# Which two loads have plain rows: the first batch's or the last batch's

## The chip, the cores and the metric

One core of a Trainium2 chip runs the kernel. The metric is device time in microseconds, lower is better.

## The reference

```python
def setup_inputs():
    batch, m, k, n = 16, 512, 768, 1024
    return {"x": np.random.randn(batch, k, m).astype(np.float32),
            "y": np.random.randn(batch, k, n).astype(np.float32)}

def reference(x, y):
    return np.einsum('bkm,bkn->bmn', x, y).astype(np.float32)
```

Sixteen matrix products in float32; the kernel reads 75.50 MB and writes 33.55 MB.

## The kernel before

SyncE issues every transfer, on one queue: 16 loads of x (1.5 MB each), 16 of y (3 MB) and 16 stores (2 MB). VectorE casts what has landed to bf16, TensorE multiplies, ScalarE copies from PSUM to the output buffers. Loads have two buffers each, so the load of batch b waits for the cast of batch b - 2.

The part that the change touches is the form of a load. Rows of x are 12 KB per partition in HBM and lie one behind the other, so four partitions' rows make one run of 48 KB; for y, two rows of 24 KB do. A **plain** load names 128 rows on both sides; a **wide** one names 32 or 64 source runs of 48 KB and still 128 destination rows. The ordinary call makes a plain load; the wide ones are built by hand from it:

```python
    made = {}
    def wide_dma(key, dst, src, dram_rows, load):
        if key not in made:                       # batch 0: plain rows
            made[key] = nc.sync.dma_start(dst, src)
            return made[key]
        pat = mybir.BassSymbolicTensorAccessPattern
        widen = lambda a: a.rearrange("(q r) k m -> q (r k m)", r=dram_rows)
        plain = lambda a: a.rearrange("p k m -> p (k m)")
        s, d = (widen(src), plain(dst)) if load else (plain(src), widen(dst))
        return nc.sync.add_instruction(_copy.replace(
            made[key].ins, name=nc.get_next_instruction_name(),
            ins=(...), outs=(...), sync_info=None, ant_dge_precooked=False))
    ...
    def load(b):
        i = b % 2
        if b >= 2:
            nc.sync.wait_ge(cast, nx[b - 2])
        wide_dma("x", xs[i][:], x_v[b], 4, True).then_inc(sx[i], 16)
        if b >= 2:
            nc.sync.wait_ge(cast, nx[b - 2] + parts(b - 2))
        wide_dma("y", ys[i][:], y_v[b], 2, True).then_inc(sy[i], 16)
    ...                                           # cut
```

## Time and profile before

| what | before | from |
|---|---|---|
| time, median of the runs beside the changed kernel | 260.73 us (260.63 to 260.77) | runs |
| span in the profile | 259.0 us | page |
| share of the 16 DMA engines, main queue | 98.5% | page, part 3 |
| busiest compute engine: PE | 69% | page, part 1 |
| first issue: start, duration | 0.95, 0.39 us | timeline |
| first packet of any engine starts | 1.97 us | packet records |
| x, then y of batch 0 done on the middle engine | 6.54, 13.87 us | packet records |
| last data packet ends | 257.72 us | packet records |
| x of batch 0, y of batch 0, last store complete, mean of the 16 engines | 6.49, 13.85, 256.44 us | packet records |

How to read it: "page" is the printed summary of a profile; its lines and the timeline are shown and read in the prediction. The last rows place the streams of packets in time, one stream on each of the 16 DMA engines; the middle engine is the one in the middle of the 16 by time. The packet records list each DMA packet's start, size and duration; no view prints them, so they stand here as numbers. Each engine closes each transfer with a completion packet of 4 bytes, and the times of completion are those of these packets.

### The profile page before, as it was taken

The page shows a single profiled execution, that of the slowest core. Times are in us where ns is not written, and L with a number is a line of the kernel's source. Part 1 is how long each engine was busy: PE and PEld are TensorE (multiplying, and loading weights), DVE is VectorE, ACT ScalarE, POOL GpSimd, SP SyncE. Part 2 cuts the span into 40 slices and gives each one's busy share as a digit, 9 for nine tenths or more (in the row PEclk, how much of TensorE's full clock was granted, in tenths as well). Part 3 has the DMA queues.
Part 4 walks back from the last instruction along what each step waited for, and adds up shares of the span by engine and source line. Part 5 has one row for each costly group of instructions (what it writes and reads, how often), then busy time and mean ns, then how long its engine had stood idle before and what let it go on. Part 6 is the DMA issues. An engine that isn't in the chain of part 4 may idle for free. (4 is left out here: it accounts for less than half of the span.)

```text
span 259.0 us, 2506 instructions
## 1 busy us (share of the span) xinstructions
PE 179.0 (69%) x768; PEld 88.9 (34%) x768; DVE 82.0 (32%) x33; ACT 60.9 (24%) x33; POOL 0.2 (0%) x4
## 2 busy tenths in 40 slices
PE   0009999999999006999069999595008999969500
PEld 0004555554545002454025555252003555534200
DVE  0261645527164350002245263300242536410000
ACT  1000342244220005222202241433000234052300
POOL 0000000000000000000000000000000000000000
PEclk9999999999999855899759999999555999988965
DMA  7999989899999999999999998999999999999995
GB/s 270 428 490 395 471 380 478 380 471 395 456 402 448 387 428 425 433 463 456 410 440 410 440 448 377 435 423 463 471 387 471 395 456 410 395 428 438 423 435 240
DMA packets 4514, 109.07 MB, mean 421 GB/s; under 512 B 768, under 2 KB 768, under 8 KB 768
## 3 DMA queue, kind: packets, MB, share of 16 engines
q1 hardware_dynamic: 4512, 109.05, 98.5%
q14 instruction: 2, 0.02, 0.0%
HBM read 75.50 MB, written 33.55 MB: 421 GB/s over the span
## 5 line engine op out<-in xcount | busy, mean ns | idle before, releaser
L154 PE MATMUL ps<-yb,xb 128*128 x768 | 179.0, 397 | 64.3 <-PEq L149 64.3
L154 PEld LDWEIGHTS ps<-yb,xb 128*128 x768 | 88.9, 116 | 154.0 <-issue 82.6
L170 ACT COPY ob<-ps 128x2048 f32<-128x2048 f32 x32 | 59.6, 1872 | 179.0 <-PE ps L154 139.9
L132 DVE CAST yb<-ys 128x6144 bf16<-128x6144 f32 (+1 forms) x17 | 53.8, 3171 | 77.2 <-DMA ys<-in_y_dram 77.2
L128 DVE CAST xb<-xs 128x3072 bf16<-128x3072 f32 x16 | 28.2, 1760 | 68.3 <-DMA xs<-in_x_dram 53.7
L170 ACT ACT_TABLE_LOAD x1 | 1.3, 1283 | 5.3 <-issue 5.3
L200 POOL MEMSET const-bfloat16-1.0<- 128x1 bf16 x1 | 0.1, 103 | 0.0
L200 POOL MEMSET const-uint8-127<- 128x1 uint8 x1 | 0.1, 103 | 0.0
L200 POOL MEMSET const-float32-0.0<- 128x1 f32 x1 | 0.1, 99 | 0.2 <-issue 0.2
L200 POOL MEMSET const-float32-1.0<- 128x1 f32 x1 | 0.1, 99 | 0.0
## 6 DMA issues: line engine op xcount, KB each, us to landing
ys<-in_y_dram SPq DMA_DIRECT2D x16, 3072.0 KB, 18.6
out_dram<-ob SPq DMA_DIRECT2D x16, 2048.0 KB, 26.3
xs<-in_x_dram SPq DMA_DIRECT2D x16, 1536.0 KB, 20.1
```

Source lines behind the costliest of these rows:

```text
L128: nc.vector.tensor_copy(xb[:, i], xs[i][:]).then_inc(cast, 1)
L132: nc.vector.tensor_copy(yb[:, i, ks], ys[i][:, ks]).then_inc(cast, 1)
L154: mm = nc.tensor.matmul(ps[g][:, m, nt], x_w[:, bass.ds(s, 1), kt, mo], yb[:, bass.ds(s, 1), kt, nt * NF:(nt + 1) * NF], start=(kt == 0), ...
L170: cp = nc.scalar.copy(ob[b % NO][:, g * HB:(g + 1) * HB].rearrange("p m (t f) -> p m t f", f=NF), ps[g][:])
L200: nc = _bacc.Bacc("TRN2", target_bir_lowering=False, num_devices=1)
```

## The change

Its intent is to let the very first loads have 48 KB runs too. Two plain loads must remain, and they become those of the last batch.

```diff
-    made = {}
-    def wide_dma(key, dst, src, dram_rows, load):
-        if key not in made:
-            made[key] = nc.sync.dma_start(dst, src)
-            return made[key]
+    def load_dma(b, dst, src, rows):
+        if b == B - 1:
+            return nc.sync.dma_start(dst, src)
+        s = src.rearrange("(q r) k m -> q (r k m)", r=rows)
+        d = dst.rearrange("p k m -> p (k m)")
         pat = mybir.BassSymbolicTensorAccessPattern
...                                               # cut
+        return nc.sync.add_instruction(mybir.InstDMACopy(
+            mode="Copy", name=nc.get_next_instruction_name(),
+            engine=nc.sync.engine, queue="qSPDynamicHW",
             ins=(...), outs=(...)))
...                                               # cut
-        wide_dma("x", xs[i][:], x_v[b], 4, True).then_inc(sx[i], 16)
+        load_dma(b, xs[i][:], x_v[b], 4).then_inc(sx[i], 16)
```

More of the change, by code (lines that the diff above doesn't have):

```diff
@@ L3 @@
 _os.environ.setdefault("NEURON_RT_ULTRASERVER_MODE", "4")
-import copy as _copy
 from contextlib import ExitStack
@@ L65 @@
     outs = ec(nc.semaphore("outs"))
-    made = {}
-    def wide_dma(key, dst, src, dram_rows, load):
-        if key not in made:
-            made[key] = nc.sync.dma_start(dst, src)
-            return made[key]
-        pat = mybir.BassSymbolicTensorAccessPattern
-        widen = lambda a: a.rearrange("(q r) k m -> q (r k m)", r=dram_rows)
-        plain = lambda a: a.rearrange("p k m -> p (k m)")
-        s, d = (widen(src), plain(dst)) if load else (plain(src), widen(dst))
-        return nc.sync.add_instruction(_copy.replace(
-            made[key].ins, name=nc.get_next_instruction_name(),
+    def load_dma(b, dst, src, rows):
[3 more added lines that the diff above has]
+        d = dst.rearrange("p k m -> p (k m)")
+        pat = mybir.BassSymbolicTensorAccessPattern
+        return nc.sync.add_instruction(mybir.InstDMACopy(
+            mode="Copy", name=nc.get_next_instruction_name(),
+            engine=nc.sync.engine, queue="qSPDynamicHW",
             ins=(pat(ap=s.ap, dtype=s.dtype, bass_ap=s, is_dma=False),),
-            outs=(pat(ap=d.ap, dtype=d.dtype, bass_ap=d, is_dma=False),),
-            sync_info=None, ant_dge_precooked=False))
+            outs=(pat(ap=d.ap, dtype=d.dtype, bass_ap=d, is_dma=False),)))
     def parts(b):
@@ L106, in load @@
             nc.sync.wait_ge(cast, nx[b - 2])
-        wide_dma("x", xs[i][:], x_v[b], 4, True).then_inc(sx[i], 16)
+        load_dma(b, xs[i][:], x_v[b], 4).then_inc(sx[i], 16)
         if b >= 2:
             nc.sync.wait_ge(cast, nx[b - 2] + parts(b - 2))
-        wide_dma("y", ys[i][:], y_v[b], 2, True).then_inc(sy[i], 16)
+        load_dma(b, ys[i][:], y_v[b], 2).then_inc(sy[i], 16)
     loads, stores = iter(range(B)), iter(range(B - 1))
```

## The prediction

> **What bounds the kernel now.** I read the page first, for who is busy. Its first, second and third parts answer at once:
>
> ```profile
> PE 179.0 (69%) x768; PEld 88.9 (34%) x768; DVE 82.0 (32%) x33; ACT 60.9 (24%) x33; POOL 0.2 (0%) x4
> ...
> DMA  7999989899999999999999998999999999999995
> GB/s 270 428 490 395 471 380 478 380 471 395 456 402 448 387 428 425 433 463 456 410 440 410 440 448 377 435 423 463 471 387 471 395 456 410 395 428 438 423 435 240
> DMA packets 4514, 109.07 MB, mean 421 GB/s; under 512 B 768, under 2 KB 768, under 8 KB 768
> ...
> q1 hardware_dynamic: 4512, 109.05, 98.5%
> ```
>
> No compute engine is busy for more than 69% of the 259.0 us span, while the 16 DMA engines are busy for 98.5% of it; the only slices under 8 tenths are the first (7) and the last (5). The chain that ended last is of no use here: it covers 5% PE and 1% ACT, because it follows instructions and the end of this kernel is a transfer. The packet counts also tell how the transfers are cut. There are 48 transfers and 768 = 48 x 16 tiny packets, so each transfer runs on all 16 engines and ends with one completion write on each. The other 4512 - 768 = 3744 are data: 16 stores x 128 rows of 16 KB = 2048; batch 0, loaded with plain rows, 128 of 12 KB (x) and 128 of 24 KB (y) = 256; the 15 other batches, with 48 KB source runs, 32 (x) and 64 (y) each = 1440. The sum fits exactly.
>
> Next, the timeline of the first and the last microseconds, for the transfer instructions (SPq). Columns: start, duration, what.
>
> ```profile
> 0.95 0.39 SPq L74 DMA_DIRECT2D xs<-in_x_dram  x1
> 1.39 0.42 SPq L74 DMA_DIRECT2D ys<-in_y_dram  x1
> 1.86 0.54 SPq L74 DMA_DIRECT2D xs<-in_x_dram  x1
> 2.44 0.65 SPq L74 DMA_DIRECT2D ys<-in_y_dram  x1
> ...
> 7.14 1.76 DVE L128 CAST xb<-xs 128x3072 bf16<-128x3072 f32 x1 [7.14 <-DMA xs<-in_x_dram]
> 8.93 0.47 SPq L74 DMA_DIRECT2D xs<-in_x_dram  x1
> 15.05 3.36 DVE L132 CAST yb<-ys 128x6144 bf16<-128x6144 f32 x1 [6.14 <-DMA ys<-in_y_dram]
> 18.43 0.47 SPq L74 DMA_DIRECT2D ys<-in_y_dram  x1
> ```
> ```profile
> 223.98 3.43 DVE L132 CAST yb<-ys 128x3072 bf16<-128x3072 f32 x2 [3.51 <-DMA ys<-in_y_dram]
> ...
> 243.33 1.87 ACT L170 COPY ob<-ps 128x2048 f32<-128x2048 f32 x1 [3.26 <-PE ps L154]
> 249.08 0.33 SPq L185 DMA_DIRECT2D out_dram<-ob  x1
> ```
>
> The reader should see four loads issued back to back, then one more each time a cast frees a buffer. Is the queue ever empty? The trace also lists each DMA packet with its start, size and duration; I strung them together into 16 serial streams, one an engine. On the middle engine every later transfer was issued 9 us or more before the engine reached it (the load of y for batch 2: issued by 18.90, reached at 28.43). Only the last store is closer: issued by 249.41, reached at 251.47. The streams have no hole but a few of 0.3 us beside instruction fetches. So **the end is the start of the first packet plus the length of one in-order stream per engine**, about 255 us. First packets start at 1.97 us (the last engine's at 2.80), last data packets end between 255.8 and 257.7 us.
>
> **What the Trainium skill says.** (1) "DMA: Bandwidth & Descriptors", section "Queues, rings and completion order": on each engine, descriptors are consumed in ring order. The trace agrees: the streams follow the order of issue. (2) Same page, "How many engines (k)", under the section on why a DMA adds 16 to its semaphore: the largest k up to 16 that divides the slowest dimension of both patterns. 32 and 64 source rows against 128 partitions still give 16, and the 768 completion writes agree, so the wide form loses no engine. (3) Same page, "Why small descriptors are slow": a fixed overhead of about 3 cycles per packet inside the DMA engine. The packet records show a fixed part: median 460 ns for 12,288 B and 912 ns for 24,576 B, a straight line with 452 ns per 12,288 B and 8 ns fixed. It predicts 8 + 4 x 452 = 1816 ns for 49,152 B; the undisturbed ones take 1815. At these sizes 8 ns is 2% at most. (4) Same page, "Specifications": about 0.6 us to the first byte for a transfer issued from SP. Here the first issue ends at 0.95 + 0.39 = 1.34 and the first packet starts at 1.97: 0.63 us.
>
> **The change part by part.** The order of instructions stays: 48 transfers on one queue with the same waits. Nothing else moves on any engine. What differs is two plain loads, which go from the first two places to the last two load places, and two wide ones, which go the other way. The totals of packets of each size are the same.
>
> - Batch 0 becomes wide. Per engine, x goes from 8 x 460 = 3.68 us to 2 x 1.815 = 3.63 us; y from 8 x 912 = 7.30 to 4 x 1.815 = 7.26. Saved: 0.05 + 0.04 = **0.09 us**, at the head of every stream, so on the path.
> - Batch 15 becomes plain. The wide packets there have a median of 1829 ns, so 6 x 1.829 = 10.97 us now. Plain packets in the same mode: some of batch 0 that ran beside 1841 to 1848 ns wide ones took 465 and 920 ns, so 8 x 0.465 + 8 x 0.920 = 11.08. Added: **0.11 us**, ahead of the last six stores, so on the path too.
> - The first issue. Plain loads took 0.39 and 0.42 us to issue, unhurried wide ones 0.47. The first packet can only come after its issue: **+0.08 us**. For batch 15 issue time is hidden: the queue is over 9 us ahead.
> - The start. The 128 packets of 12 KB have a mean of 530 ns against a median of 460, all of it in the first two rounds (first packets 0.66 to 1.32 us). (530 - 460) x 128 / 16 = **0.56 us** per engine is start-up. If it is a latency, one per engine, the wide form pays the same once and the change is 0. If it is paid per packet, two wide packets pay about as much as the two first plain ones. I take 0, with 0.3 us either way.
>
> Sum: -0.09 + 0.11 + 0.08 + 0 = +0.10 us on 260.71: 260.8 us.
>
> What lies beside other work: x of batch 0 lands for the cast at 7.14 and would do so within 0.2 us; TensorE starts after y of batch 0 and its cast, at 18.99. Even half a microsecond there would be worth nothing, as no load waits that closely on the compute. At the end, the last ACT copy is done at 243.33 + 1.87 = 245.20, and the last store is issued at 249.08: 3.9 us of slack for a later landing of batch 15.
>
> **The rivals.**
> 1. *Wide runs start the kernel faster, and this shows.* For it: fewer, longer source reads in the phase in which all 16 engines start cold, and 0.56 us is lost there. Against: that is all there is to win. Halved: -0.3 us, so 260.4; none left: 260.2, a 0.2% gain.
> 2. *Wide runs start it slower.* A 48 KB packet can start only when the engine has its descriptors, and starts are staggered from 1.97 to 2.80 us already. If the stagger doubles, +0.8 us at most on the late engines, but those are not the ones that end last: +0.4, so 261.1.
> 3. *A wait at the end takes over.* Plain rows let the last y land differently, and the casts, matmuls and stores of batch 15 come later. The 3.9 us above speaks against it, as does that the store of batch 9 and not the load frees ACT at 228.87. It would take a landing 4 us late. Time: unchanged.
> 4. *Uneven engines.* One engine ends at 257.7 and the median at about 256.4; the slow one lost about 1 us in scattered hiccups beside instruction fetches and completions. Longer packets at the time of the early fetches could shift who is late: 0.5 us either way, and that is also the noise between executions of one kernel in one profile. The three timed runs spread over 0.14 us only.
>
> **Range and chances.** The sure terms are tenths of a microsecond and cancel; the unsure ones are the start (0.3) and the unevenness (0.4), together about 0.5. Range 260.3 to 261.3. 2% would be 5.2 us; nothing in the trace has that size except a queue that runs dry, and it is at least 9 us ahead. So within 2%: 0.98.
>
> **What would show it.** Right: the same 4514 packets with 98% or more DMA share; first packets at about 2.05 us; the first x cast at 7.0 to 7.3 and the first y cast at 14.8 to 15.3; issue of the first load 0.47 us; the last y cast within 0.3 us of 223.98; the last store issued within 0.5 us of 249.08. Wrong: first packets of 48 KB that take well over 1.8 + 0.6 us; a first cast that moves by over 0.5 us and an end that moves with it; plain packets at the end slower than 465 and 920 ns; or a hole in the streams.

## More of the kernel before

In the built program, what the ordinary call makes (plain loads and stores) carries a flag, `ant_dge_precooked`; what is built by hand does not. Below, a transfer with the flag is called *marked*.

## The result, and the profile after

The changed kernel takes **261.18 us** (261.15 to 261.30, four runs) against 260.73 us before: +0.45 us by the medians, a ratio of 1.0019 with an interval of 1.0001 to 1.0036. Ratios here are the mean time of one kernel's fast runs over that of the other's fast runs of the same rounds, so not quite the ratio of the medians. The result is in the predicted range of 260.3 to 261.3 and in the class "within 2%", and the loss is over four times the predicted 0.10 us.

The page of the changed kernel, busy times, packet counts and queue:

```profile
PE 178.6 (69%) x768; PEld 88.9 (34%) x768; DVE 82.0 (32%) x33; ACT 60.9 (23%) x33; POOL 0.2 (0%) x4
...
DMA packets 4515, 109.07 MB, mean 420 GB/s; under 512 B 769, under 2 KB 769, under 8 KB 769
...
q1 hardware_dynamic: 4512, 109.05, 98.4%
```

The main queue has the same 4512 packets and the same bytes (the one more packet is on the queue for instructions), and nearly the same share of a slightly longer span. So next to nothing was added to the streams; they lie later. The timeline of the changed kernel shows where, at the head (columns: start, duration, instruction):

```profile
0.95 0.55 SPq L75 DMA_DIRECT2D xs<-in_x_dram  x1
1.55 0.57 SPq L75 DMA_DIRECT2D ys<-in_y_dram  x1
2.17 0.60 SPq L75 DMA_DIRECT2D xs<-in_x_dram  x1
2.81 0.61 SPq L75 DMA_DIRECT2D ys<-in_y_dram  x1
...
7.77 1.76 DVE L123 CAST xb<-xs 128x3072 bf16<-128x3072 f32 x1 [7.77 <-DMA xs<-in_x_dram]
9.56 0.47 SPq L75 DMA_DIRECT2D xs<-in_x_dram  x1
15.44 3.36 DVE L127 CAST yb<-ys 128x6144 bf16<-128x6144 f32 x1 [5.90 <-DMA ys<-in_y_dram]
```

and at the tail:

```profile
196.72 0.35 SPq L71 DMA_DIRECT2D xs<-in_x_dram  x1
...
205.55 0.34 SPq L71 DMA_DIRECT2D ys<-in_y_dram  x1
...
224.15 3.43 DVE L127 CAST yb<-ys 128x3072 bf16<-128x3072 f32 x2 [4.85 <-DMA ys<-in_y_dram]
...
249.53 0.33 SPq L180 DMA_DIRECT2D out_dram<-ob  x1
```

The first issue starts at 0.95 as before and takes 0.55 us instead of 0.39. The first cast of y starts 0.39 us later (15.44 against 15.05), the last store is issued 0.45 us later (249.53 against 249.08), the span is 0.4 us longer. By the packet records, the first packet starts at 2.28 instead of 1.97 us. Averaged over the 16 engines, x of batch 0 is complete at 6.93 instead of 6.49 us, y of batch 0 at 14.29 instead of 13.85 and the last store at 256.86 instead of 256.44: 0.43 to 0.45 us later at each. A shift that is whole after the first transfer and no larger at the end was made at the head. (Single casts show it less well, as each waits for the slowest engine of its transfer: the last cast of y is only 0.17 us later, 224.15 against 223.98.)

### The profile page after: what moved, and what is told of

It is laid out like the page before. It is cut to its first block, busy times and chain, and to the rows that moved or that the text cites. A ratio compares the mean times of both kernels' runs of the same rounds, so it can differ in the third digit from the quotient of the medians.

```text
span 259.4 us, 2506 instructions
## 1 busy us (share of the span) xinstructions
PE 178.6 (69%) x768; PEld 88.9 (34%) x768; DVE 82.0 (32%) x33; ACT 60.9 (23%) x33; POOL 0.2 (0%) x4
## 3 DMA queue, kind: packets, MB, share of 16 engines
q1 hardware_dynamic: 4512, 109.05, 98.4%
```

## The experiments

My theory after this comparison, **H**: the time was lost ahead of the first packets and kept to the end, because no stream is ever empty. Its rivals: **T**, the plain rows of the last batch cost it; **C**, compute starts later and never catches up. H itself splits: **H1**, the form of the issue (marked or not) delays the start; **H2**, the 48 KB runs do. Ten kernels were run: nine ask a question, and the last is a version meant to be faster. All gave correct results, each was timed in five rounds beside the kernel before on the same chip. Kernels are compared only within the same rounds. The expectations name absolute times, so a few were missed by up to 0.11 us (experiments 1, 2, 4, 9 and 10); what counts is the difference from the kernel before.

### 1. Plain rows at both ends

```diff
# against the changed kernel
-        if b == B - 1:
+        if b in (0, B - 1):
```

> Batches 0 and 15 both plain, the rest wide. Theory H (the 0.45 us are lost at the head of the streams, before the first packets): 260.7 to 260.85, first packet at 1.97, middle engine done with x of batch 0 at about 6.5. Rival T (the plain rows of the last batch cost it): 261.1 to 261.2.

Measured: 260.65 us against 260.57, ratio 1.0002 (0.9989 to 1.0016); first packet at 1.97 us, x of batch 0 done at 6.58. The plain rows of the last batch alone cost nothing that can be seen. T falls.

### 2. The plain batch in the middle

A kernel without any plain load did not build: the compiler refused the hand-made load of y with "physical tensor cannot be Function argument and cannot be NEFF IO". I read this as each input needing one ordinary load somewhere, and that is why the change moves the plain rows and does not drop them. So they went to batch 7.

```diff
# against the changed kernel
-        if b == B - 1:
+        if b == 7:
```

> Batch 0 wide as in the changed kernel, last batch wide as in the kernel before, the one plain batch is number 7. Theory H: 261.1 to 261.25, first packet at 2.28. Rival T: 260.7 to 260.8.

Measured: 261.00 us against 260.57, ratio 1.0015 (1.0002 to 1.0029); first packet at 2.28 us. With the tail wide as it was before the change, the loss is still there. Together with the first experiment: the head makes it, the tail does not.

### 3. Plain rows at the head, without the mark

```diff
# against the kernel before
+    nc.dge_precook = False          # ordinary calls make unmarked transfers
     ...                             # cut
     for nl, ns in TURNS:
         for b in islice(loads, nl):
             load(b)
+            nc.dge_precook = True   # from the second batch on as before
```

> The kernel before, plain rows in batch 0, but the two first loads are issued without the mark that plain loads carry in the built program, as the wide ones are. Splits theory H. H1 (the form of the issue delays the start): issue about 0.55 us, first packet at about 2.25, time 261.05 to 261.2. H2 (the 48 KB runs delay it): issue 0.39 or a little more, first packet at 1.97 to 2.05, time 260.7 to 260.8.

Measured: 261.09 us against 260.57, ratio 1.0020 (1.0006 to 1.0034). Its timeline:

```profile
0.94 0.54 SPq L74 DMA_DIRECT2D xs<-in_x_dram  x1
1.54 0.58 SPq L74 DMA_DIRECT2D ys<-in_y_dram  x1
```

Every run length in this kernel is that of the kernel before; only the mark is gone from two instructions. The issue takes 0.54 us, the first packet (12 KB) starts at 2.26 us, and the time is that of the changed kernel. H2 falls, H1 stands: **the run length has no visible part in the loss; the missing mark on these two loads makes it.**

### 4. Only x of batch 0 back to plain

```diff
# against the changed kernel
-        if b == B - 1:
+        if b == B - 1 or (b == 0 and rows == 4):   # rows is 4 for x, 2 for y
```

> The changed kernel with x of batch 0 alone back to plain rows; y of batch 0 stays wide, batch 15 plain. Theory H with only the very first transfer mattering: 260.65 to 260.8, first packet at 1.97. If y's issue at the head matters as well (it queues behind x's): about 260.95.

Measured: 260.59 us against 260.57, ratio 1.0000 (0.9986 to 1.0014). One transfer restored, and all of the loss is gone, with y of batch 0 still wide. Its timeline:

```profile
0.95 0.39 SPq L71 DMA_DIRECT2D xs<-in_x_dram  x1
1.39 0.53 SPq L75 DMA_DIRECT2D ys<-in_y_dram  x1
```

The unmarked issue of y takes 0.53 us here, and nobody pays for it: it ends at 1.92 us, and the middle engine is done with x only at 6.59 us.

### 5. Only x of batch 0 unmarked

```diff
# against the kernel before, in load(b)
+        nc.dge_precook = b > 0      # off for x of batch 0
         ...                         # cut
         wide_dma("x", xs[i][:], x_v[b], 4, True).then_inc(sx[i], 16)
         ...                         # cut
+        nc.dge_precook = True       # on for y
```

> The kernel before with the mark taken from the first x load alone; the first y load and all stores keep it. Theory H1 (one issue is all of it): first packet at about 2.26, time 260.95 to 261.15, as with both unmarked. If the second issue had a part: between 260.7 and 260.9.

Measured: 261.08 us against 260.74, ratio 1.0012 (0.9998 to 1.0026): the medians are 0.34 us apart, and every one of its runs (261.05 to 261.13) is above every run of the kernel before (260.69 to 260.85), though the interval of the ratio just touches 1. First packet at 2.35 us. It was meant as the mirror of experiment 4, but one thing was not as meant:

```profile
0.95 0.55 SPq L74 DMA_DIRECT2D xs<-in_x_dram  x1
1.55 0.57 SPq L74 DMA_DIRECT2D ys<-in_y_dram  x1
```

The issue of y took 0.57 us, as long as an unmarked one, though the edit turns its mark on again. So in its first two issues this run repeats experiment 3 (0.54 and 0.58); it does not isolate the first issue, and it says nothing about marked issues behind unmarked ones. That the very first issue is what counts rests on experiments 3 and 4 together: slow issues of x and y lose the time, a slow issue of y alone does not.

### 6. The mark taken from all stores

```diff
# against the kernel before
         for b in islice(loads, nl):
             load(b)
+            nc.dge_precook = False  # from here on every ordinary call is unmarked
```

> The kernel before with the mark taken from all stores; only the two plain loads of batch 0 keep it. Theory H1 (only the first issue is on the path, all later ones are hidden behind the queue): stores take some 0.5 us to issue instead of 0.33, time 260.5 to 260.7. Rival (each unmarked issue costs some 0.3 us wherever it stands): over 262.

Measured: 260.52 us against 260.63, ratio 0.9998 (0.9985 to 1.0012). The view of the store line in this kernel (columns: minimum/median/maximum in ns, first and last start in us), then in the kernel before:

```profile
L101 SPq DMA_DIRECT2D out_dram<-ob x15: 472/596/600, 73.8 to 232.1; - x15
```
```profile
L101 SPq DMA_DIRECT2D out_dram<-ob x15: 332/430/586, 73.9 to 232.6; - x15
```

Sixteen stores were issued more slowly, by 0.14 us where no other issue stands just ahead (the minima), and the time did not move: these issues are made far ahead of the engines. Even the last store, only 2 us ahead, had room.

### 7. The head 0.63 us later

```diff
# against the kernel before, ahead of the first load
+    for _ in range(10):
+        nc.sync.sem_inc(idle, 1)
```

> The kernel before with ten semaphore increments on SyncE ahead of its first load, to move the first issue later by some tenths of a microsecond. Theory H1 (a delay of the first packet goes to the end one for one, since no stream is ever empty): the time grows by as much as the first packet moves, for a first issue at 1.4 some 0.45 us, 261.0. Rival (the start is hidden, the queue being ahead by 9 us): 260.6.

Measured: 261.58 us against 260.63, ratio 1.0033 (1.0020 to 1.0047). The first issue now starts at 1.58 us:

```profile
1.58 0.39 SPq L74 DMA_DIRECT2D xs<-in_x_dram  x1
```

The first packet starts at 2.63 us, 0.66 later than before; the span of the profile is 0.7 us longer, and the ratio makes +0.86 us of 260.63, with an interval of 0.52 to 1.22. So a delay of the head is paid in full. It seems to be paid with a little more, as in the changed kernel (0.31 us for the first packet, 0.45 us in the time). Part of that surplus is in the measure: the first packet is that of the quickest engine alone. Averaged over the 16 engines, x of batch 0 is complete 0.73 us later here and 0.45 us later in the changed kernel; what is left lies within the interval.

### 8 and 9. Compute later, transfers as before

Twenty semaphore increments on VectorE hold back the first cast of x in the one kernel and the first cast of y in the other.

```diff
# against the kernel before; the second kernel has the same behind wait_ge(sy[i], n)
         nc.vector.wait_ge(sx[i], n)
+        if b == 0:
+            for _ in range(20):
+                nc.vector.sem_inc(idle, 1)
```

> The kernel before with twenty semaphore increments on VectorE between the landing of the first x and its cast, so that the first cast, and what follows it, comes later by about as much as in the changed kernel or more. Theory H1: unchanged, 260.5 to 260.7. Rival C (the changed kernel is slower because compute starts later): 261.0 or more.

> The kernel before with twenty semaphore increments on VectorE between the landing of the first y and its cast, some 2 us: TensorE starts about 2 us later, at 21 instead of 19. Theory H1: unchanged, 260.5 to 260.7. Rival C (the later start of compute costs the time): 261 to 262.6.

Measured: 260.58 us against 260.63 (ratio 0.9995, 0.9982 to 1.0009) for x, and 260.76 us against 260.74 (ratio 1.0001, 0.9987 to 1.0015) for y. The timeline of the second:

```profile
16.88 3.36 DVE L135 CAST yb<-ys 128x6144 bf16<-128x6144 f32 x1 [7.56 <-issue]
...
20.82 4.45 PE L157 MATMUL ps<-yb,xb 128*128 x10 [20.82 <-PEq L152]
```

TensorE starts at 20.82 us, 1.83 us later than before (18.99), and the time does not move. In the changed kernel it starts at 19.37, only 0.38 us later. C falls. The first kernel of the two held the cast of x back by 2.05 us (9.19 against 7.14), and with it the issue of the third x load, for nothing as well.

### 10. The first load ahead of the scheduler's section

If a later head is paid in full, an earlier head should be a gain. By the instruction records of the kernel before, SyncE leaves the start barrier at about 0.67 us and spends the time to 0.95 us on entering the section in which all else stands. This version issues the first x load, plain and marked, ahead of that section.

```diff
# against the kernel before; xs0, sx0 and the transfer are handed to the kernel function
+        x0_dma = nc.sync.dma_start(xs0[:], args[0].rearrange("b (p ko) m -> b p ko m", ko=6)[0])
+        x0_dma.then_inc(sx0, 16)
         with _tile.TileContext(nc) as tc:
...
+        if b > 0:
             wide_dma("x", xs[i][:], x_v[b], 4, True).then_inc(sx[i], 16)
```

> The kernel before with the first x load (plain rows, marked) issued ahead of the scheduler's section, right after the start barrier. Theory H1: the first issue comes at about 0.7 instead of 0.95, the first packet at about 1.7, and the end comes as much earlier: 260.3 to 260.4, faster than both kernels. Rival (the head of the stream is hidden): 260.6.

Measured: 260.51 us (260.40 to 260.52) against 260.74 (260.69 to 260.85), ratio 0.9989 (0.9976 to 1.0003). The head of its timeline:

```profile
0.73 0.38 SPq L217 DMA_DIRECT2D xs<-in_x_dram  x1
1.39 0.33 SPq L76 DMA_DIRECT2D ys<-in_y_dram  x1
```

The issue comes 0.22 us earlier, the first packet at 1.74 instead of 1.97 us, and the median is 0.23 us lower. All five runs lie below all nine of the kernel before, while the interval of the ratio still reaches 1; so a gain of a tenth of a per cent is likely and not settled. Its profile does not settle it either: the first packet is 0.23 us earlier, but averaged over the 16 engines x of batch 0 is complete only 0.02 us earlier than in the profile before, and kernels with an unchanged first load lie 0.01 to 0.18 us later than that one. It was run with the kernel before and not with the changed one; against that, the two differences add up to about 0.7 us.

| kernel | first packet against before | x of batch 0 complete, mean of 16 engines, against before | time against before (medians) |
|---|---|---|---|
| changed | +0.31 us | +0.45 us | +0.45 us |
| 1, plain at both ends | 0 | +0.07 | +0.08 |
| 2, plain in the middle | +0.31 | +0.30 | +0.43 |
| 3, plain head, unmarked | +0.29 | +0.42 | +0.52 |
| 4, x of batch 0 plain | +0.03 | +0.04 | +0.02 |
| 5, x of batch 0 unmarked | +0.38 | +0.48 | +0.34 |
| 6, stores unmarked | -0.01 | +0.01 | -0.11 |
| 7, head delayed | +0.66 | +0.73 | +0.95 |
| 8 and 9, casts delayed | 0 | +0.01 and +0.18 | -0.05 and +0.02 |
| 10, first load early | -0.23 | -0.02 | -0.23 |

The first two columns come from one profile each, the last from four or five timed runs. The kernels whose first load is unmarked (changed, 2, 3, 5) stand apart from those whose first load is as before (1, 4, 6, 8, 9) in every column.

## Why the prediction was right or wrong

**The bound: right.** The streams of packets set the end, compute has room, and the wait at the end never takes over. Experiments 8 and 9 show that compute has room, 7 that the start of the streams is paid at the end, 6 that later issues are hidden, and 1 that plain rows at the end wake no other wait.

**Batch 0 becomes wide, -0.09 us: right in kind, too small to be seen.** Steady wide packets took 1815 ns as counted. Within batch 0's x the gain was eaten by the start: the 128 plain packets take 128 x 529.6 / 16 = 4.24 us per engine, start-up included, and the two wide ones 4.30 us. For y it is 7.32 us instead of 7.35.

**Batch 15 becomes plain, +0.11 us: right sign, too large.** The plain packets there have means of 464 and 916 ns, so 8 x 0.464 + 8 x 0.916 = 11.04 us. The wide ones of batch 15 before had means of 1845 ns (x) and 1828 (y), so 2 x 1.845 + 4 x 1.828 = 11.00 us. That is +0.04 us, and experiment 1 cannot tell it from zero. The prediction used one median, 1829 ns, for both, and its 920 ns for y rested on two packets.

**The first issue, +0.08 us: this is the term that was mis-sized.** I took 0.47 us for an unmarked issue from later, lone ones; the first in the kernel takes 0.55, so +0.16 us. And I let the mark pass as a detail of the form, where it was the thing that the change moved. The time from the end of the issue to the first packet, which the prediction took to stay at 0.63 us, grew with it: 1.97 - 1.34 = 0.63 us with the mark, 2.28 - 1.50 = 0.78 without. That is another 0.15 us, and it is the same in experiment 3 with 12 KB rows (2.26 - 1.48 = 0.78), and 0.85 in experiment 5 (2.35 - 1.50); the other kernels with a marked first load have 0.63 to 0.66. In sum +0.31 us, for the quickest engine, for the term that I put at 0.08.

**The start, 0 with 0.3 either way: right that a latency is paid once.** Above the steady 1815 ns, the first wide packets lost a mean of 0.66 us, against 0.56 us before; the second ones ran at full pace. So start-up is neither halved nor doubled by longer runs.

Added up with measured terms, as means of the 16 engines: x of batch 0 is complete 0.45 us later, of which its packets are 4.30 - 4.24 = 0.06 and the later start of the streams the other 0.39; its y gives 7.32 - 7.35 = -0.03 and batch 15 gives +0.04. In all that is +0.46 us, against +0.45 us measured; agreement closer than some 0.1 us would be chance, as one profile differs from the next by that much.

That the time fell into the range is in part luck. The range was made of 0.3 us for the start-up of packets and 0.4 us for uneven engines; none of it was meant for the mark, which took most of it.

**The rivals.** The second came closest, with 261.1 us and "starts it slower"; its mechanism, an engine that must wait for the descriptors of a 48 KB packet, falls with experiment 3. The first was wrong: no gain at the start. The third stayed out, as argued. The fourth, uneven engines, stays as noise: in each of the two profiles the last engine ends about 1.3 us behind the middle one (257.72 against 256.38, 258.18 against 256.91).

**What would show it.** The last cast of y within 0.3 us of 223.98 (224.15) and the last store within 0.5 us of 249.08 (249.53) were right. The first issue of 0.47 (0.55), the first packets at about 2.05 (2.28) and the first y cast at 14.8 to 15.3 (15.44) were missed by the one term. So was the first x cast at 7.0 to 7.3 (7.77), but there chance has a part: with an unchanged first load it came anywhere from 7.10 (experiment 4) to 7.60 (experiment 1). And a sign of being wrong came true, a first cast that moves by over 0.5 us (0.63) with an end that moves along (0.45); by the y cast and the completions above it was the head that moved.

Left open: why the mark shortens an issue and what follows it, which no profile shows, and whether a wide load with the mark would start as fast. The mark was not put on wide loads, as nothing here says whether that form may carry it.

## What to carry to other kernels

When the transfers form one stream that never runs dry, look for what lies ahead of its first packet: a delay there was paid at the end (experiments 3 and 7), while slower issues of y and of the stores, or first casts 2 us later, were free here. Give the first transfer the form that is quickest to issue; issuing it earlier probably gains too. Choose the form of all others by what the engines make of it. All of this was worth 0.2% or less here. And read in a diff what moves besides what its words name: here it spoke of run lengths and moved a flag.

## What the Trainium skill lacked or had wrong

- "DMA: Bandwidth & Descriptors", section "Specifications", has one figure for the first byte of a transfer issued from SyncE, about 0.6 us, and does not say from where it counts. From the end of the first issue to the first packet the runs show 0.63 to 0.66 us for a marked one and 0.78 to 0.85 us for an unmarked one. No page has the mark, nor that it shortens the issue itself: 0.39 against 0.55 us for the first, 0.33 against 0.47 us for a lone store.
- The same page, section "Why small descriptors are slow", gives the fixed cost of a packet as about 3 cycles, without a time for it on large packets. Fitted to 12 and 24 KB packets here it is 8 ns, so that 48 KB runs save 2% at most, and moving two of 32 loads between the forms saves nothing that can be seen.
- The same page, section "Where 436 GB/s comes from", says that for transfers between HBM and SBUF the HBM side, about 358 GB/s, binds. With one core at work the whole kernel, loads and stores together, moved 421 GB/s on average. That fits the page's own measurement of 425 GB/s for a single core's 16 MB load; the sentence lacks the condition that the page gives beside that measurement, both cores of the pair streaming.
